# Fourier front: a root and a scaled table per tile, odd features' sums inside the eight-row products, ten tile operations on GpSimd

## The chip, the core and the metric

The program runs on one core of a Trainium2 chip. A core has engines with a queue of instructions each, which wait for one another by semaphores: TensorE (PE; its weight loads are listed as PEld) multiplies matrices into PSUM, VectorE (DVE), ScalarE (ACT) and GpSimd (POOL) work on tiles in SBUF, the first two on PSUM as well. DMAs are issued from the queues of SyncE (SP), ScalarE and GpSimd. PSUM holds eight tiles of 128x512, and a pool hands them out in turn. The metric is device time in microseconds, the median of repeated runs.

## What is computed

Two sequences of 512 rows by 1024 features pass through two layers: a Fourier mixer with an MLP, then attention with an MLP. The change touches the first mixer alone:

```python
def fourier_mix(h, w_out):
    hg = h.astype(jnp.float32).reshape(B, S, N_FGROUPS, F_GROUP)      # 8 groups of 128 features
    f = jnp.fft.fft2(hg, axes=(1, 3), norm="ortho").real
    return f.reshape(B, S, D_MODEL).astype(h.dtype) @ w_out

x = x + fourier_mix(rms_norm(x, fourier_norm[j]), fourier_w_out[j])
```

`rms_norm` divides each row by the root of its mean square and multiplies by a gain per feature.

## The kernel before, in words

The transform over positions and the one over features are products with cosine and sine tables. By symmetry of the tables an input tile of 128 rows by 1024 features (its features are laid out in two mirrored halves of 512) is replaced by the sum (`plus`) and the difference (`minus`) of its halves. A class `Front(q, c)` does this for tiles 2c and 2c+1 of sequence q: `squares` (ScalarE, sum of squares of a row), `gain` (times the gain row `gr`), `plus`, `minus`, `chain` (six small steps to the reciprocal root `r`), then scaling by `r`, and `combine`, which joins two tiles whose rows are mirrored in the sequence.

Sequence 0 comes first, with nothing to hide its start, so it uses exact f32 products: `transform(0)` multiplies three such parts (`parts[k]`: sum, difference, and a small tile for the Nyquist rows) with tables `cosX[k]`, `sinX[k]` in three rounds of `exact_even`, `exact_odd` and `exact_nyq`. `seq_evac` copies the results to SBUF, `feat_stage` multiplies by the feature tables and splits the result into a high and a low part (`split`: ScalarE copies the high half in the rounded type, VectorE subtracts it to get the low one). `an` holds the eight rows of the alternating features; `en` collects four small products (L554) for the features at multiples of 64.

The mixer's weights come as four pairs of 128x1024 tiles (`Fold`). `minus` forms their difference on VectorE, and an accumulating DMA adds the second to the first in place (L647). Differences are split into `wo` (`odd`), sums into `we` (`even_hi`, `even_lo`). `odd_outs(0)` then fills all eight PSUM tiles in four rounds over `wo`, eight outputs in each; `even_outs(0)` makes one output after another from `we[0..3]` and a small tile. Meanwhile the second sequence is prepared: `g0` and `g1` are its `Front`s, `plus_there` adds halves by an accumulating DMA on GpSimd's queue (L420), and `table(k)` loads four tables on the same queue (L329). `transform(1)` follows on TensorE, with split operands (`seq_part`, `feat_stage`), and then the same outputs for sequence 1. After it the MLP's products begin.

The order on every engine is the order of the code: the region stands under a manual schedule, and each engine runs its instructions as they are written. `idle(o, n)` puts n filler products on TensorE.

Of the kernel before, what the change touches and what calls it, by code (L numbers as in the profile page):

```python
# [44 lines left out]
def trunk_kernel(ctx, tc, x_in, xt_in, y_out, tables, rope, gfour, gcol, grow, gfin,  # L45
# [296 lines left out]
    def begin():  # L342
# [5 lines left out]
        for t in range(2, 4):  # L348
            load_x(0, t)
        exact_table(5)  # L350
        exact_table(6)
        nc.scalar.activation(one[:, :1], one[:, :1], AF.Sqrt)
        idle(ps(), 8)
        halves = []
        for i in range(2):
            o = ps()
            for k in range(4):
                c = 4 * i + k
                nc.tensor.transpose(o[:, k * P : (k + 1) * P], g[:, c : c + 1].broadcast_to([P, P]), ident)  # L359
            nc.scalar.copy(gr[:, i * 512 : i * 512 + 512], o)  # L360
            halves.append(o)
# [30 lines left out]
    def eights(x):  # L392
        return x[:, 0:512:64].unsqueeze(1).broadcast_to([P, 5, 8])

    class Front:


        def __init__(self, q, c):
            self.q, self.c = q, c
            self.ss, self.r = small(2), small(2)  # L400
            self.steps = rsqrt_steps(self.r[:, :2], self.ss[:, :2], 2, 1.0 / D)
            self.xg, self.p, self.m = [None] * 2, [None] * 2, [None] * 2
# [4 lines left out]
        def gain(self, i, k=None, o=None):  # L407
# [3 lines left out]
            nc.vector.tensor_mul(self.xg[i][:, sl], xa[self.q, 2 * self.c + i][:, sl], gr[:, sl] if o is None else o)  # L411
# [25 lines left out]
        def scale_both(self, i):  # L437
            if i == 0:
                self.n = sm.tile([P, 2, 5, 8], F32, tag="ny", name=nm("ny"), bufs=2, padded_shape=[P, 2, 8, 8])
            for out, x in ((self.p[i], self.p[i]), (self.n[:, i], eights(self.m[i])), (self.m[i], self.m[i])):  # L440
                nc.scalar.activation(out, x, AF.Copy, scale=self.r[:, i : i + 1])  # L441
            parts.append((self.p[i], self.m[i], self.n[:, i]))

        def combine(self):
            (p1, p2), (m1, m2), r, w = self.p, self.m, self.r, 8
            stt = nc.vector.scalar_tensor_tensor
            if self.q == 0:
                n = sm.tile([P, 5, 8], F32, tag="ny", name=nm("ny"), bufs=2, padded_shape=[P, 16, 8])
                stt(n, eights(m2), r[:, 1:2], eights(m1), ALU.mult, ALU.add)
# [60 lines left out]
    def exact_nyq(k, o):  # L510
        nc.tensor.matmul(o[0:40, :258], parts[k][2].rearrange("p a b -> p (a b)"), cosX[k], start=k == 0, stop=k == 2)
# [26 lines left out]
    def feat_nyq(u, j, first):  # L538
        nyt = nyqs[0][:, j * P : (j + 1) * P]
        nc.tensor.matmul(u[:, :258], nyt, an, start=first, stop=not first)  # L540
        return u

    def feat_stage(q, j, a, b, an, en, u=None):
        if q == 0:
            nc.tensor.matmul(u[:, :258], ftX[:, :P], a, start=False, stop=True)
        else:
            u = ps()
            mm3(u[:, :258], ft(0)[:, 0:P], ft(1)[:, 0:P], a[:, 0], a[:, 1], True, False)
            feat_nyq(u, j, False)
        v = ps()  # L550
        pick = slice(6 - 2 * j, 78 - 2 * j)
        if q == 0:
            nc.tensor.matmul(v[:, :256], ftX[:, P:], b, start=True, stop=True)
            nc.tensor.matmul(en[0:72, :258], pickX[:, pick], a, start=j == 0, stop=j == 3)  # L554
        else:
            mm3(v[:, :256], ft(0)[:, P:], ft(1)[:, P:], b[:, 0], b[:, 1], True, True)
            ent = tabs[2][:, 516:594][:, pick]
            nc.tensor.matmul(en[0:72, :258], ent, a[:, 0], start=j == 0, stop=False)
            nc.tensor.matmul(en[0:72, :258], ent, a[:, 1], start=False, stop=j == 3)
# [4 lines left out]

    def nyq_out(q, en):
        t = slot([P, 258], F32R)[0:72]
        nc.scalar.copy(t, en[0:72, :258])
        nc.vector.tensor_sub(t[64:72], en[64:72, :258], f32(t[64:72]))
        un[q] = t
# [9 lines left out]
    def transform(q, mid=lambda: None, hook=lambda at, j: None):  # L579
        on, ov = ps(), [(ps(), ps()) for _ in range(3)]  # L580
        if q == 0:
            for k in range(2):
                for j in range(3):
                    exact_even(k, j, ov[j][0])
                exact_nyq(k, on)
                for j in range(3):
                    exact_odd(k, j, ov[j][1])
            mid()
            exact_nyq(2, on)
        else:  # L590
            seq_nyq(q, 0, on)
            for j in range(3):
                seq_part(q, j, 0, *ov[j])
            mid()
            seq_nyq(q, 1, on)
        en = ps()
        nc.scalar.copy(an[0:40], on[0:40, :258])
        nc.vector.tensor_sub(an[32:40], on[32:40, :258], f32(an[32:40]))
        ab = []
        for j in range(3):  # L600
            if q == 0:
                exact_odd(2, j, ov[j][1])
                exact_even(2, j, ov[j][0])
            else:
                seq_part(q, j, 1, *ov[j])
            ab.append(seq_evac(q, *ov[j]))
            hook("seq", j)
        us = [None] * 4
        if q == 0:
            us[0] = feat_nyq(ps(), 0, True)  # L610
        feat_stage(q, 0, *ab[0], an, en, us[0])
        hook("feat", 0)
        o3 = ps(), ps()
        if q == 0:
            for k in range(3):
                exact_even(k, 3, o3[0])
            for k in range(3):
                exact_odd(k, 3, o3[1])
        else:
            for c in range(2):  # L620
                seq_part(q, 3, c, *o3)
        ab.append(seq_evac(q, *o3))
        hook("seq", 3)
        if q == 0:
            us[1:] = [feat_nyq(ps(), j, True) for j in range(1, 4)]
        feat_stage(q, 1, *ab[1], an, en, us[1])
        hook("feat", 1)
        feat_stage(q, 2, *ab[2], an, en, us[2])
        hook("feat", 2)
        feat_stage(q, 3, *ab[3], an, en, us[3])  # L630
        nyq_out(q, en)
        hook("feat", 3)

# [3 lines left out]
    class Fold:  # L637
# [7 lines left out]
        def minus(self):  # L645
            nc.vector.tensor_sub(self.b, self.a, self.b)
            nc.gpsimd.dma_start(self.a, w_four[1, self.j], accum_op=ALU.add)  # L647

        def odd(self):
            hi, lo = lent()  # L650
            split(hi, lo, self.b)
            wo.append((hi, lo))
# [5 lines left out]
        def even_lo(self):  # L658
            w = self.w
            nc.vector.tensor_sub(w[1], self.a, f32(w[0]))  # L660
            we[self.j] = w

    class FoldNyq:


        def __init__(self):
            self.w = slot([P, D], F32R)[0:72]
# [3 lines left out]
        def load(self):  # L671
# [7 lines left out]
            for r, i in ((0, 0), (32, 1), (64, 0)):  # L679
# [21 lines left out]
    def even_outs(q, fos):  # L701
        return outs(q, fos, we, 0, 258, (wn.w, un[q]))
# [31 lines left out]
    with tc.manual_schedule(engines={ET.PE, ET.Activation, ET.DVE, ET.Pool, ET.SP}):  # L734
        gr, halves_gr = begin()
        gc = cons.tile([P, 4 * KC], F32, name="gc")
        cosX = [exact[0][:, :258], exact[0][:, 514:772], exact[1][:, 256:514]]
        sinX = [exact[0][:, 258:514], exact[1][:, :256], exact[1][:, 514:770]]
        ftX, pickX = exact[2][:, :256], exact[2][:, 256:334]
        f0, f1, wn = Front(0, 0), Front(0, 1), FoldNyq()  # L740
        wn.load()
        idle(ps(), 28)
        f0.squares(0)
        for k in range(2):
            f0.gain(0, k, halves_gr[k])
        f0.minus(0)
        f0.plus(0)
        f0.squares(1)
        f0.gain(1, 0)
        f0.chain(0, 6)  # L750
        f0.scale_both(0)
        f0.gain(1, 1)
# [1368 lines left out]
```

## Time and profile before

| | us |
|---|---|
| median of 3 runs | 1672.69 (1672.32 to 1673.72) |
| the profiled execution's own time | 1671.97 |
| its span, first to last instruction | 1670.2 |
| TensorE busy | 1659.8 (99%) |
| VectorE busy | 1264.1 (76%) |
| ScalarE busy | 871.9 (52%) |
| GpSimd busy | 393.0 (24%) |

A row of the timeline gives the start in us from the start of the span, the duration, the engine, the line, what is written and read, and in brackets the engine's idle time ahead of it and what ended it. An f32 product counts as two instructions on TensorE (x6 is three products). Rows of neighbouring instructions are merged (x8). Names like `u`, `t`, `s` are pools: `u` the slots of 4 KB per partition, `t` the 2 KB ones, `s` small columns, `ps` PSUM.

### The profile page before, as it was taken

To read this page: it belongs to the slowest core of one execution; us is meant where nothing else is said; L and a number is where in the kernel's file an instruction comes from. 1 tells how busy PE (TensorE), PEld (TensorE's weight loads), DVE (VectorE), ACT (ScalarE), POOL (GpSimd) and SP (SyncE) were. 2 spreads that over 40 slices of the span, in tenths; PEclk is the share of its full clock that TensorE was granted. 3 is DMA by queue.
4 is the path that set the end of the run, shared out by engine and by line. 5 is a ranking of instruction groups with operands and counts; after the bars stand their busy time and mean duration, and the time that the engine had idled before them with its cause. 6 is when DMAs were issued, how large, how long until landed. Compare 5 with 4: busy or idle time off the path is not lost.

```text
span 1670.2 us, 22258 instructions
## 1 busy us (share of the span) xinstructions
PE 1659.8 (99%) x7828; PEld 1385.6 (83%) x7828; DVE 1264.1 (76%) x1851; ACT 871.9 (52%) x1540; POOL 393.0 (24%) x364
## 2 busy tenths in 40 slices
PE   9999999999999999999999999999999999999998
PEld 7988888888888888888888888888888888888887
DVE  8879776557786869869888877777855487878875
ACT  7776444446342425447688855554454552433334
POOL 3321444221000001324554303004422220000002
PEclk9999999999999999999999999999999999999999
DMA  9843555459775757425401146334544695757532
GB/s 304 259 158 115 207 192 180 145 177 370 247 232 166 247 174 230 172 77 195 161 5 38 64 177 226 114 120 171 208 146 167 223 375 193 233 157 232 183 103 101
DMA packets 122192, 302.48 MB, mean 181 GB/s; under 512 B 12344, under 2 KB 13496, under 8 KB 122080
## 3 DMA queue, kind: packets, MB, share of 16 engines
q1 hardware_dynamic: 98720, 253.53, 43.7%
q0 software_dynamic: 8960, 21.05, 5.9%
q10 hardware_dynamic: 14400, 26.48, 4.2%
q8 instruction: 61, 1.00, 0.2%
q14 instruction: 51, 0.42, 0.1%
HBM read 217.59 MB, written 82.38 MB: 180 GB/s over the span
## 4 chain that ended last, share of the span: by engine, by line
PE 98%; DVE 1%; ACT 1%; DMA 0%; issue 0%; POOL 0%; DVEq 0%; POOLq 0%
PE ps L940 75%; PE ps L83 6%; PE ps L81 6%; PE ps L82 6%; PE ps L1535 2%; PE ps L1514 0%; PE ps L191 0%; PE ps L508 0%; PE ps L505 0%; DMA g<-gfour 0%; PE ps L199 0%; ACT t L130 0%; ACT t L441 0%; DVE u L1919 0%; PE ps L359 0%
## 5 line engine op out<-in xcount | busy, mean ns | idle before, releaser
L940 PE MATMUL ps<-u,w 128*128 128x512 f32 x4944 | 1130.8, 389 | 0.0
L940 PEld LDWEIGHTS ps<-u,w 128*128 128x128 f32 x4944 | 926.8, 188 | 194.4 <-ACT u L973 1.7
L86 ACT CAST w<-raw 128x1024 fp32r<-128x1024 f32 (+1 forms) x216 | 213.6, 994 | 308.6 <-PE ps L940 230.2
L87 DVE TENSOR_TENSOR w<-raw,w 128x1024 fp32r<-128x1024 f32 (+1 forms) x216 | 251.2, 1167 | 75.6 <-ACT w L86 75.4
L86 ACT CAST u<-u 128x1024 fp32r<-128x1024 f32 x144 | 145.0, 1048 | 85.1 <-PE ps L940 37.1
L87 DVE TENSOR_TENSOR u<-u,u 128x1024 fp32r<-128x1024 f32 x144 | 173.4, 1232 | 16.9 <-ACT u L86 16.0
L940 PE MATMUL ps<-u,u 128*128 128x512 f32 x600 | 143.2, 389 | 0.0
L1150 DVE TENSOR_TENSOR u<-ps,u 128x512 f32<-128x512 f32 x160 | 109.3, 685 | 38.1 <-PE ps L940 35.6
L1177 POOL DMA_DIRECT2D raw<-w_sum x32 | 27.7, 865 | 468.9 <-DMA raw<-w_sum 158.0
L1058 POOL TENSOR_TENSOR u<-u 128x512 f32<-128x512 f32 x28 | 38.0, 1355 | 424.3 <-ACT u L955 424.3
L940 PEld LDWEIGHTS ps<-u,u 128*128 128x128 f32 x600 | 112.6, 188 | 23.8 <-ACT u L973 0.4
L81 PE MATMUL ps<-u,u 128*128 128x512 f32 (+2 forms) x340 | 128.7, 380 | 0.0
L83 PE MATMUL ps<-u,u 128*128 128x512 f32 (+2 forms) x340 | 123.7, 365 | 0.0
L82 PE MATMUL ps<-u,u 128*128 128x512 f32 (+2 forms) x340 | 123.6, 365 | 0.0
L182 POOL TENSOR_TENSOR t<-t,t 128x512 f32<-128x512 f32 (+1 forms) x54 | 79.2, 1470 | 186.7 <-ACT t L178 185.7
L954 ACT ACTIVATE t<-t 128x512 f32<-128x512 f32 x64 | 40.4, 632 | 110.0 <-DVE t L1027 100.0
L83 PEld LDWEIGHTS ps<-u,u 128*128 128x128 f32 x340 | 64.2, 189 | 10.5 <-DVE u L87 0.2
L87 DVE TENSOR_TENSOR u<-ps,u 128x512 fp32r<-128x512 f32 (+3 forms) x112 | 68.0, 634 | 5.6 <-ACT u L86 5.0
L82 PEld LDWEIGHTS ps<-u,u 128*128 128x128 f32 x340 | 64.4, 189 | 8.5 <-DVE u L87 0.3
L81 PEld LDWEIGHTS ps<-u,u 128*128 128x128 f32 x340 | 64.4, 189 | 7.8
L1014 DVE TENSOR_TENSOR t<-ps,u 128x512 f32<-128x512 f32 x32 | 22.0, 687 | 60.7 <-PE ps L940 56.9
L86 ACT CAST u<-ps 128x512 fp32r<-128x512 f32 (+3 forms) x112 | 59.2, 555 | 7.5 <-PE ps L1535 6.1
(270 smaller groups left out, 2013.7 us busy)
## 6 DMA issues: line engine op xcount, KB each, us to landing
raw<-w_up SPq DMA_DIRECT2D x80, 512.0 KB, 4.6
u<-spill_t SPq DMA_DIRECT2D x60, 512.0 KB, 7.1
raw<-w_sum SPq DMA_DIRECT2D x56, 512.0 KB, 5.6
u<-spill_b SPq DMA_DIRECT2D x45, 512.0 KB, 6.2
spill_t<-u SPq DMA_DIRECT2D x84, 256.0 KB, 2.0
spill_b<-t ACTq DMA_DIRECT2D x60, 256.0 KB, 4.3
raw<-w_row SPq DMA_DIRECT2D x28, 512.0 KB, 4.8
park<-u SPq DMA_DIRECT2D x24, 512.0 KB, 4.5
```

The costliest lines, as they stand in the source:

```text
L81: nc.tensor.matmul(out, lh, rh, start=first, stop=False)
L82: nc.tensor.matmul(out, lh, rl, start=False, stop=False)
L83: nc.tensor.matmul(out, ll, rh, start=False, stop=last)
L86: hi = nc.scalar.copy(dst_hi, src)
L87: return hi, eng.tensor_sub(dst_lo, src, f32(dst_hi))
L182: nc.gpsimd.tensor_add(acc[q][:, :n], acc[q][:, :n], s[:, :n])
L940: nc.tensor.matmul(o, w[x][:, sl], h[k][y], start=first and k + i == 0, stop=k == n - 1 and i == 2, skip_group_check=not first)
L954: nc.scalar.activation(t, src, AF.Relu)
L1058: eng.tensor_sub(t[:, 0], b12, b11)
L1150: return nc.vector.tensor_add(x, o, x)
L1177: nc.gpsimd.dma_start(s[:, 1], w[:, 3], accum_op=ALU.add)
L1535: nc.tensor.transpose(pt[:, t * P : (t + 1) * P], probs[t][:, sc * P : (sc + 1) * P], ident)
```

## The change

For the first two tiles of sequence 0 the roots are computed one by one, and each root scales its table (`exact[i]`, rows of the table belong to rows of the tile) instead of the tile's sum and difference; the tables are laid out anew so that each tile has its own. The first tile's gain is read from PSUM before the gain row is copied. All four column blocks now run in one round, so there are 4 + 4 products per round. The Nyquist tile gets 24 more columns with sums of the odd features over each group of 64 (VectorE reduces, ScalarE spreads them), so that one product of 56 rows gives both `an` and the low rows `un[0]`; the four products into `en` go for sequence 0. GpSimd multiplies the third and fourth tile of sequence 0 and all four of sequence 1 by the gain (those were VectorE's), and it adds the weights (that was a DMA). The tables of sequence 1 are loaded later in the code, fold tiles and inputs earlier; twelve and twenty fillers replace eight and 28.

```diff
-        idle(ps(), 8)
+        idle(ps(), 12)
...
-            nc.scalar.copy(gr[:, i * 512 : i * 512 + 512], o)
...
+    def nyq_tiles(n):
+        t = sm.tile([P, n, 2, 4, 8], F32, tag="ny", name=nm("ny"), bufs=2, padded_shape=[P, 2, 2, 4, 8])
+        return [t[:, i] for i in range(n)]
+    def odd_sums(k):
+        s = small(8)
+        x = parts[k][0].rearrange("p (g d i) -> p g d i", g=8, i=2)[:, :, :, 1]
+        nc.vector.tensor_reduce(s, x, AX.X, ALU.add)
+        return s
+    def put_sums(k, s):
+        nc.scalar.copy(parts[k][2][:, :, 1:], s.unsqueeze(1).unsqueeze(1).broadcast_to([P, 2, 3, 8]))
...
-            nc.vector.tensor_mul(self.xg[i][:, sl], xa[self.q, 2 * self.c + i][:, sl], gr[:, sl] if o is None else o)
+            eng.tensor_mul(self.xg[i][:, sl], xa[self.q, 2 * self.c + i][:, sl], gr[:, sl] if o is None else o)
...
-            for out, x in ((self.p[i], self.p[i]), (self.n[:, i], eights(self.m[i])), (self.m[i], self.m[i])):
-                nc.scalar.activation(out, x, AF.Copy, scale=self.r[:, i : i + 1])
+        def table(self, i):
+            t = exact[i][:, :514]
+            nc.scalar.activation(t, t, AF.Copy, scale=self.r[:, i : i + 1])
...
+    def put_low(on):
+        norm = 1.0 / math.sqrt(S * P)
+        low = slot([P, 258], F32R)[0:56]
+        nc.scalar.activation(low, on[0:56, :258], AF.Copy, scale=norm)
+        nc.vector.scalar_tensor_tensor(low[32:56], on[32:56, :258], norm, f32(low[32:56]), ALU.mult, ALU.subtract)
+        un[0] = low
...
+    def transform_exact(mid, hook):
+        ov = [(ps(), ps()) for _ in range(4)]
+        for k in range(2):
+            for j in range(4):
+                exact_even(k, j, ov[j][0])
+            for j in range(4):
+                exact_odd(k, j, ov[j][1])
+        mid()
+        ab = []
+        for j in range(4):
+            exact_odd(2, j, ov[j][1])
+            exact_even(2, j, ov[j][0])
+            ab.append(seq_evac(0, *ov[j]))
+            hook("seq", j)
+        on = ps()
+        for k in range(3):
+            exact_nyq(k, on)
+        put_an(on)
+        put_low(on)
...
-            nc.vector.tensor_sub(self.b, self.a, self.b)
-            nc.gpsimd.dma_start(self.a, w_four[1, self.j], accum_op=ALU.add)
+            nc.vector.tensor_sub(self.d, self.a, self.b)
+        def plus(self):
+            nc.gpsimd.tensor_add(self.a, self.a, self.b)
...
-        idle(ps(), 28)
+        idle(ps(), 20)
+        f0.table(0)
...
+        f1.gain(0, eng=nc.gpsimd)
+        f1.gain(1, eng=nc.gpsimd)
...
+        for i in range(2):
+            g0.gain(i, eng=nc.gpsimd)
+        for j in range(4):
+            fold[j].even_hi()
         fold[0].even_lo()
         fold[1].even_lo()
+        g0.minus(1)
+        g0.plus_there(1)
+        fold[2].even_lo()
+        fold[3].even_lo()
+        g1.gain(0, eng=nc.gpsimd)
...
+        g1.gain(1, eng=nc.gpsimd)
...
         even(0)
+        g0.combine()
+        g0.split_even()
+        g0.split_odd()
...
         g1.minus(1)
         g1.plus_there(1)
+        for k in range(4):
+            table(k)
```

Where instructions move, engine by engine. VectorE in the front, from the first tile's sum on (`t_199`/`t_205` is a sum, `u_203`/`u_248` the second tile times its gain, `s` the root's small columns). Before:

```order
L415 TENSOR_TENSOR t_199<-u_194 128x512
L411 TENSOR_TENSOR u_203<-u_104,u_99 128x512
L141 TENSOR_SCALAR s_141<-s_139 128x2
L143 RECIPROCAL s_142<-s_143 128x2
L144 TENSOR_TENSOR s_144<-s_142 128x2
L145 SCALAR_TENSOR_TENSOR s_144<-s_144,s_141 128x2
L146 SCALAR_TENSOR_TENSOR s_140<-s_144,s_142 128x2
L411 TENSOR_TENSOR u_203<-u_104,u_99 128x512
```

And now:

```order
L146 SCALAR_TENSOR_TENSOR s_140<-s_144,s_142 128x1
L433 TENSOR_TENSOR t_205<-u_193 128x512
L442 TENSOR_TENSOR t_207<-u_193 128x512
L429 TENSOR_TENSOR u_248<-u_104,u_99 128x1024
L141 TENSOR_SCALAR s_145<-s_139 128x1
L143 RECIPROCAL s_146<-s_147 128x1
L144 TENSOR_TENSOR s_148<-s_146 128x1
L145 SCALAR_TENSOR_TENSOR s_148<-s_148,s_145 128x1
L146 SCALAR_TENSOR_TENSOR s_140<-s_148,s_146 128x1
L433 TENSOR_TENSOR t_262<-u_248 128x512
```

The first root stands ahead of the first tile's sum and difference, and the second root behind the second tile's whole gain product.

VectorE between the last odd weights and the first even output (`w` are the even weights' low halves, `t_416`/`t_540` and `t_423`/`t_560` the differences of the second sequence's first two tiles). Before:

```order
L87 TENSOR_TENSOR u_409<-u_301,u_408 128x1024
L411 TENSOR_TENSOR u_414<-u_304,u_99 128x1024
L424 TENSOR_TENSOR t_416<-u_414 128x512
L411 TENSOR_TENSOR u_421<-u_306,u_99 128x1024
L424 TENSOR_TENSOR t_423<-u_421 128x512
L141 TENSOR_SCALAR s_244<-s_242 128x2
L143 RECIPROCAL s_245<-s_246 128x2
L144 TENSOR_TENSOR s_247<-s_245 128x2
L145 SCALAR_TENSOR_TENSOR s_247<-s_247,s_244 128x2
L146 SCALAR_TENSOR_TENSOR s_243<-s_247,s_245 128x2
L660 TENSOR_TENSOR w_536<-raw_234,w_536 128x1024
L660 TENSOR_TENSOR w_538<-raw_238,w_538 128x1024
```

And now:

```order
L689 TENSOR_TENSOR u_425<-u_418,u_424 128x1024
L442 TENSOR_TENSOR t_540<-u_432 128x512
L141 TENSOR_SCALAR s_160<-s_158 128x2
L143 RECIPROCAL s_161<-s_162 128x2
L144 TENSOR_TENSOR s_163<-s_161 128x2
L145 SCALAR_TENSOR_TENSOR s_163<-s_163,s_160 128x2
L146 SCALAR_TENSOR_TENSOR s_159<-s_163,s_161 128x2
L701 TENSOR_TENSOR w_550<-raw_221,w_550 128x1024
L701 TENSOR_TENSOR w_552<-raw_227,w_552 128x1024
L442 TENSOR_TENSOR t_560<-u_434 128x512
L701 TENSOR_TENSOR w_554<-raw_231,w_554 128x1024
L701 TENSOR_TENSOR w_556<-u_235,w_556 128x1024
```

The gain products (L411) left VectorE; the differences that read them stayed ahead of the even halves, the second one between them.

GpSimd's queue from the weights to the tables (`raw` are weight tiles, `u_414`, `u_421` and now `u_432` to `u_573` the second sequence's tiles, `dcos` and the rest its tables). Before:

```order
L647 DMA raw_296<-w_four 128x1024
L647 DMA u_300<-w_four 128x1024
L420 DMA u_414<-u_414 128x512
L420 DMA u_421<-u_421 128x512
L431 TENSOR_TENSOR s_544<-s_243,mask 128x1
L455 MEMSET ny_570 128x128
L329 DMA u_579<-dcos 128x774
L329 DMA u_581<-dsin 128x1024
```

And now:

```order
L429 TENSOR_TENSOR u_434<-u_241,u_99 128x1024
L438 DMA u_432<-u_432 128x512
L449 TENSOR_TENSOR s_548<-s_159,mask 128x1
L438 DMA u_434<-u_434 128x512
L429 TENSOR_TENSOR u_565<-u_243,u_99 128x1024
L429 TENSOR_TENSOR u_573<-u_245,u_99 128x1024
L438 DMA u_565<-u_565 128x512
L476 MEMSET ny_607 128x128
L438 DMA u_573<-u_573 128x512
L329 DMA u_630<-dcos 128x774
L329 DMA u_632<-dsin 128x1024
```

The four adds of weights (L682) and the second sequence's first product (L429) stand ahead of these rows. The tables now come behind all four gain products and all four adds of halves.

More of the change, by code (lines that the diff above doesn't have):

```diff
@@ L577, in idle, with put_an @@
             nc.tensor.matmul(o[:, :256], filler, filler.unsqueeze(1).broadcast_to([P, 2, P]), start=True, stop=True)
[L579 to L596, printed above, removed]
+    def put_an(on):
@@ L792, in hook0 @@
             elif j == 3:
+                fold[3].minus()
+                fold[3].plus()
+                g0.squares(1)
+                g0.chain(1, 2)
                 fold[3].odd()
[L794 to L803 removed]
+        transform_exact(mid, hook0)
```

303 lines of the change are left out of this document (154 added, 149 removed).

## The prediction

> **What bounds the kernel now.** I read the page first, then the list of what TensorE (PE) waits for, then busy time by stage, then the order of time of single engines.
>
> ```profile
> span 1670.2 us, 22258 instructions
> PE 98%; DVE 1%; ACT 1%; DMA 0%; issue 0%; POOL 0%; DVEq 0%; POOLq 0%
> ```
>
> ```profile
> PE ps L505 <- ACT t L441: 1.4, 2, 1.0
> ```
>
> ```profile
> 0.00:10.60 10.60, 7.81 (x45) 7.35 (x45) 4.99 (x18) 5.82 (x11) 1.84 (x8) 1.00 0.81 313
> 10.60:29.55 18.95, 18.55 (x82) 13.75 (x83) 18.68 (x30) 14.67 (x33) 8.16 (x10) 1.00 1.04 372
> 29.55:41.26 11.71, 11.71 (x99) 11.68 (x98) 10.77 (x18) 10.01 (x18) 5.54 (x9) 1.00 1.01 189
> 41.26:54.00 12.74, 12.74 (x109) 12.73 (x108) 12.13 (x25) 9.85 (x31) 4.16 (x6) 1.00 0.67 160
> ```
>
> The chain that ends last is PE for 98%. In the Fourier front PE waits 1.4 us for scaled sums and from then on for nothing. The windows give length, then busy time of PE, weight loads, DVE (VectorE), ACT (ScalarE), POOL (GpSimd). VectorE is busy 18.68 of 18.95 us, 10.77 of 11.71 and 12.13 of 12.74: the second limit lies right behind the first. So whatever holds VectorE up in the first 57 us moves PE; after the front the program is PE-bound and its order unchanged, so a shift at the second transform stays to the end.
>
> ```profile
> 1.18 2.07 PE L577 MATMUL ps<-u 128*128 128x256 f32 x8 [1.18 <-DVE mask L370]
> 3.84 1.94 PE L359 MATMUL ps<-ident,g 128*128 128x128 f32 x8 [0.59 <-DMA g<-gfour]
> 5.43 4.15 PE L577 MATMUL ps<-u 128*128 128x256 f32 x28
> 10.60 1.57 PE L505 MATMUL ps<-u,t 128*128 128x258 f32 x6 [1.01 <-ACT t L441]
> ...
> 22.87 1.47 PE L505 MATMUL ps<-u,t 128*128 128x258 f32 x6
> 24.17 1.46 PE L508 MATMUL ps<-u,t 128*128 128x256 f32 x6
> ...
> 29.55 0.47 PE L81 MATMUL ps<-u,u 128*128 128x256 f32 x1
> ...
> 41.26 0.28 PE L81 MATMUL ps<-u,w 128*128 128x258 f32 x1
> ...
> 42.71 0.28 PE L698 MATMUL ps<-u,u 72*128 72x258 f32 x1
> ...
> 53.75 0.28 PE L81 MATMUL ps<-u,ny 128*40 128x258 f32 x1
> ```
>
> These are my checkpoints: first exact product 10.60, first odd output 29.55, first even output 41.26, end of that output 42.8, second transform 53.75. Three exact products take 1.30 us (22.87 to 24.17), one 0.43.
>
> **PE's own work.** Twelve fillers stand ahead of the transposes instead of eight: about 0.9 us more, which fills the 0.59 us wait, so the transposes come some 0.1 later. Twenty follow instead of 28; eight fast ones less, at the 0.12 us of the 96 products between 29.55 and 41.26, are 1.0 less, so PE is free at 9.6+0.1-1.0 = 8.7. The scaled table is there by then:
>
> ```profile
> 7.16 0.69 DVE L424 TENSOR_TENSOR t<-u 128x512 f32<-128x512 f32 x1
> 7.77 0.69 DVE L415 TENSOR_TENSOR t<-u 128x512 f32<-128x512 f32 x1
> 17.67 0.75 DVE L450 SCALAR_TENSOR_TENSOR t<-t,s,t 128x512 f32<-128x512 f32 x1
> 28.31 2.07 DVE L87 TENSOR_TENSOR u<-ps,u 128x257 fp32r<-128x257 f32 x6
> 36.21 0.16 DVE L141 TENSOR_SCALAR s<-s 128x2 f32<-128x2 f32 x1
> 36.94 3.49 DVE L660 TENSOR_TENSOR w<-raw,w 128x1024 fp32r<-128x1024 f32 x3
> 40.66 1.23 DVE L660 TENSOR_TENSOR w<-u,w 128x1024 fp32r<-128x1024 f32 x1 [0.23 <-ACT w L656]
> ```
>
> ```profile
> 9.82 0.72 ACT L441 ACTIVATE t<-t,s 128x512 f32<-128x512 f32 x1 [1.00 <-DVE s L146]
> ```
>
> The first half of the transposes ends near 5.0 (3.84, half of 1.94, and 0.1). VectorE's half products need no copy first and end at 5.8 and 6.6, the root's steps take 0.73 (36.21 to 36.94), the scaling 0.72: ready near 8.0. Start of the exact products: 10.60 to 8.7, **-1.9**. They number 35 instead of 39 (four e/n products, L554, go): **-1.7**; the second wait of 0.4 goes. Unhindered, odd outputs would begin near 25.5.
>
> **GpSimd's tiles and the shared access.** Ten 128x1024 products or adds of two SBUF tiles move to GpSimd: two in front, four for the weights, four for the second sequence. In front of them on its queue only memsets are left. No 128x1024 stands in the trace; these rows bound it.
>
> ```profile
> L1488 POOL TENSOR_TENSOR t<-u,u x4: 732/734/742, 865.7 to 888.7; 128x256 f32<-128x256 f32 x4
> ```
>
> ```profile
> L182 POOL TENSOR_TENSOR t<-t,t 128x512 f32<-128x512 f32 x48 | 73.3, 1530 | 179.6 <-ACT t L178 178.7
> ```
>
> ```profile
> 287.61 1.28 POOL L1059 TENSOR_TENSOR u<-t,u 128x512 f32<-128x512 f32 x1
> ```
>
> ```profile
> 156.40 1.29 POOL L1058 TENSOR_TENSOR u<-u 128x512 f32<-128x512 f32 x1 [54.43 <-ACT u L955]
> 157.77 1.62 POOL L1059 TENSOR_TENSOR u<-t,u 128x512 f32<-128x512 f32 x1
> 159.35 1.74 POOL L1060 TENSOR_TENSOR u<-t,u 128x512 f32<-128x512 f32 x1
> ```
>
> ```profile
> 157.13 1.11 DVE L989 TENSOR_TENSOR raw<-raw,raw 128x512 f32<-128x512 f32 x1
> 158.27 1.67 DVE L990 TENSOR_TENSOR raw<-raw 128x512 f32<-128x512 f32 x1
> 159.86 0.68 DVE L1027 TENSOR_TENSOR t<-ps,t 128x512 f32<-128x512 f32 x1
> ```
>
> 0.73 for 256 and 1.28 for 512 elements, so 0.55 per 256: 2.4 for 1024 (ends: 1.3, one 512 row, and 3.1, twice L182's mean; I take the value on the line through the two uncrowded rows). The last two fences interlock. VectorE's L989, of a shape that takes 0.69 (L424), ends at 158.24, 0.55 after GpSimd's first add ends (157.69). GpSimd's second ends at 159.39, 1.15 after L989. L990 ends at 159.94, again 0.55 after. L1027, one operand from PSUM, runs beside an add at its 0.68. So a VectorE operation with both operands in SBUF and a GpSimd one exclude each other, in order of asking, but for a lead of 0.14. A moved tile holds VectorE's two-operand work off for up to 2.26, twice what its own 128x1024 costs ((3.49-1.22)/2 = 1.14). The trace shows 512 columns; I take the whole instruction for 1024 too. [...]
>
> **The sum, checkpoint by checkpoint** (0.60 per 128x512 on VectorE, 0.67 with a scalar, 0.345 per PSUM split, 1.14 per 128x1024):
>
> *Front to the odd outputs.* VectorE forms the first tile's sum and difference by 8.5 (7.3 and two of 0.60). From there to the last sum of the third round VectorE has one 1.14, six 0.60, two 0.67, two roots and a small sum: 8.2, so 16.6 without GpSimd. The two tiles of 2.26 come between, about 1.2 of them beside root steps, which have no two large operands: 19.9. PE, ready at 15.8, waits some 3.4. Behind three reductions (0.4 each) and two weight differences (2.3) the first two weight adds on GpSimd end at 27.8; the first odd lower half, queued behind, ends at 28.8, the splits at 29.5. First odd output 29.5: the 4.0 saved are spent, **0.0**.
>
> *Odd outputs.* The third result's bank is freed by a split that now stands behind an odd half and a weight difference (29.5+1.2+1.1+0.3 = 32.1; PE is there at 30.1: +2.0). The seventh's stands behind the third add, which ends at 34.2, and an odd half: 35.6, +2.0. First even output 41.26 to 45.3: **+4.0**.
>
> *First even output.* VectorE's queue holds the second sequence's difference ahead of all four even halves, and that waits for GpSimd. The fourth odd half ends at 40.5; then GpSimd's two tiles run on end to 45.1; difference 0.6, root 0.7, two halves 2.3, difference 0.6, third half 1.1: 50.4; GpSimd's next tile holds access to 52.6; fourth half 53.7. End of the output 54.1 instead of 42.8: **+11.3** in all. Before, the fourth half ended at 41.9.
>
> *To the second transform.* Seven more even outputs, 1.56 each (42.71 on): 65.0.
>
> ```profile
> 38.31 1.70 POOL L329 DMA_DIRECT2D u<-dcos  x1
> 41.20 0.54 POOL L329 DMA_DIRECT2D u<-dfeat  x1
> 45.74 0.88 POOL L420 DMA_DIRECT2D u<-u  x1 [4.01 <-DVE t L424]
> ```
>
> ```profile
> u<-dcos POOLq DMA_DIRECT2D x1, 387.0 KB, 4.8
> ```
>
> The tables were issued at 38.3, 15 us ahead of use. Now they stand behind the last add of halves, which waits for a VectorE difference that stands behind the first even output's add, combine and splits (54 to 61.2); 0.9 for its issue, then 4.8: 66.9, +1.9. Behind the tables two input DMAs (0.9 each) and the memset for the second eight-row tile follow, and the even adds that free PSUM banks wait behind that: some 2 more. I take **+4.0** (ends 1 and 6). The fold's four accumulating DMAs go; PE's list of waits names none of them, so that gains nothing. ScalarE loses four scalings and gains two tables and three small copies; it is behind VectorE in every window, so I cost it at nothing (if it were the limit, a scaling is 0.72).
>
> Sum: +15.3. The span becomes 1685.5 against 1670.2; that execution took 1671.97 and the runs' median is 1672.69, so I add to the median: **1688.0 us**.
>
> **Rivals.**
> *No exclusion (0.17).* GpSimd's and VectorE's passes share access at 1024 columns. The same walk without blocks starts odd outputs at 24.8, yet the first even output still waits for a tile behind the adds, and tables still come late: +5, 1677.6. Against it: every crowded row above.
> *The clock falls (0.20).* The first eight fillers take 2.07 us where later ones need 0.12 each, so TensorE starts at half speed. In the walk PE works under a third of the time from 44 to 54. Nothing in before shows such a gap. Two stretches of 3 us at half speed once work is there again cost 1.5 each: +18.3, 1691. [...]
> *GpSimd hides (0.08).* A tile takes 1.3 or less and VectorE, rid of six 1.14 products, keeps ahead. Then 1.9+1.7+0.4 stays: 1668.7. It decides where the second sequence's first tile is done before the odd outputs end (near 37). Against it: the 256 and 512 rows already give 0.55 per 256.
> *The earlier start fails* (a late tile or root): VectorE's queue ends the waits anyway, so the sum hardly changes.
>
> **How the numbers follow.** The forecast has 0.50 (1683 to 1692); 0.05 lies between no exclusion and no change. Low is the no-exclusion case less 2, 1675.5; high is a 3.1 us tile's share (ten tiles by 0.7, half of it on the path, +3.5) with part of the clock's loss: 1694. Within 0.2% is 3.3 us, about what runs of this kernel can tell: faster 0.08, same 0.05, slower 0.87.
>
> **What would show it.** Right: VectorE two-operand rows of over 2 us beside GpSimd's 128x1024 rows near 2.4 to 3.5; first exact product near 8.7; first odd output near 29.5; first even output ending near 54; waits of PE's even products for L701 halves, and of VectorE's difference for GpSimd's L429; the tables issued after 60. Wrong: VectorE's 128x1024 rows all near 1.22, or the first even output ending before 45.

## The result, and the profile after

The changed kernel takes 1696.51 us (median of 4, 1694.94 to 1697.31) against 1673.20 for the kernel before (4 runs): a ratio of 1.0137, 95% interval 1.0125 to 1.0150, so 23.3 us slower. The forecast was 1688.0 with a range up to 1694: the direction was right, the loss half as large again as said, and outside the range. The profiled execution spans 1693.2 us against 1670.2. One run of the last kernel below (1847.63 us) and one of the kernel before beside it (2077.74) ran at a lower granted clock throughout (0.85 and 0.75) and are left out of all medians and ratios.

The chain of the kernel after that ended last, between 36 and 60 us (start, length, engine, tile, line):

```profile
37.69 2.42 POOL u L682
40.11 3.35 POOL u L429
...
43.49 2.87 DVE t L442
...
47.09 2.27 DVE w L701 x2
...
49.96 6.96 DVE w L701 x2
...
56.97 0.58 PE ps L83
```

The list of what TensorE waits for up to 115 us (total, times, longest):

```profile
PE ps L83 <- DVE w L701: 8.2, 4, 4.8
PE ps L81 <- DVE u L87: 4.1, 3, 1.9
PE ps L526 <- ACT u L457: 3.7, 2, 3.4
PE ps L598 <- DVE mask L368: 1.2, 1, 1.2
```

GpSimd's tiles (L682, L429) and VectorE's two-operand work (L442, L701) take turns, and TensorE hangs on the end of the row: 8.2 us for the even halves. The first line names the even halves' subtraction (L701), the second the splits that free PSUM tiles (L87), the third the scaled tables of the front (L457). No row names a table of the second sequence or a transfer. The same checkpoints on TensorE as in the prediction:

```profile
15.03 0.80 PE L526 MATMUL ps<-u,t 128*128 128x258 f32 x1 [3.40 <-ACT u L457]
...
29.81 0.35 PE L81 MATMUL ps<-u,u 128*128 128x256 f32 x1 [0.53 <-DVE u L87]
...
45.65 0.28 PE L81 MATMUL ps<-u,w 128*128 128x258 f32 x1
...
57.48 0.58 PE L741 MATMUL ps<-u,u 56*128 56x258 f32 x1
...
73.53 0.31 PE L81 MATMUL ps<-u,ny 128*40 128x258 f32 x1
...
113.91 0.40 PE L1002 MATMUL ps<-u,w 128*128 128x512 f32 x1
```

The last checkpoint, the first product of the MLP, stands in the kernel before at:

```profile
91.04 0.40 PE L940 MATMUL ps<-u,w 128*128 128x512 f32 x1
```

| stretch | forecast, us | profile, us |
|---|---|---|
| to the first odd output | 0.0 | +0.3 |
| odd outputs | +4.0 | +4.1 |
| first even output, to its end | +7.3 | +10.7 |
| seven more even outputs, to the second transform | +4.0 | +4.7 |
| second transform and its outputs, to the MLP | 0 | +3.1 |
| MLP and all behind | 0 | +0.1 |
| sum | +15.3 | +23.0 |

Two things in it were not in the walk. The first is the granted clock. The windows of the kernel after (length; busy time of PE, weight loads, DVE, ACT, POOL; then the clock, DMA share, GB/s):

```profile
47.60:51.00 3.40, 1.66 (x6) 1.14 (x6) 3.40 (x4) 1.71 (x6) 1.40 (x3) 0.67 0.45 77
51.00:54.50 3.50, 1.01 (x3) 0.71 (x3) 3.50 (x2) 3.50 (x10) 3.50 (x3) 0.50 0.44 75
...
57.90:61.30 3.40, 3.40 (x14) 2.94 (x13) 3.00 (x7) 1.77 (x5) 1.09 (x2) 0.50 0.47 81
61.30:64.70 3.40, 3.40 (x21) 3.06 (x21) 2.69 (x6) 1.91 (x7) 0.84 (x2) 0.84 0.01 1
```

TensorE is busy 1.66 of 3.40 us, then under a third of the time, and the clock falls to 0.50; it stays there through a full window of work and comes back during the one after (0.84 in its mean). The second: an even output takes longer even at full clock. First the kernel after, with the small product of 56 rows (L741) and its neighbours; then the kernel before, with 72 rows (L698):

```profile
65.22 0.28 PE L83 MATMUL ps<-u,w 128*128 128x258 f32 x1
65.43 0.38 PE L741 MATMUL ps<-u,u 56*128 56x258 f32 x1
65.74 0.39 PE L81 MATMUL ps<-u,w 128*128 128x258 f32 x1
65.97 0.28 PE L82 MATMUL ps<-u,w 128*128 128x258 f32 x1
...
67.38 0.38 PE L741 MATMUL ps<-u,u 56*128 56x258 f32 x1
```

```profile
44.15 0.28 PE L83 MATMUL ps<-u,w 128*128 128x258 f32 x1
44.27 0.28 PE L698 MATMUL ps<-u,u 72*128 72x258 f32 x1
44.39 0.28 PE L81 MATMUL ps<-u,w 128*128 128x258 f32 x1
```

Neighbours at full clock start 0.12 apart. Around the 56 rows the starts are 0.21, 0.31 and 0.23 apart: 0.39 more, 1.95 per output instead of 1.56. The 48 rows of the second sequence cost the same (starts at 88.79, 89.00, 89.31 and 89.54), and 16 outputs make 6.2 us. No engine waits in it, so no list of waits shows it; only the rows of the two kernels side by side do.

### The profile page after: what moved, and what is told of

It reads as the page before. It is cut to its first block, busy times and chain, and to the rows that moved or that the text cites. A ratio compares the mean times of both kernels' runs of the same rounds, so it can differ in the third digit from the quotient of the medians.

```text
span 1693.2 us, 22245 instructions
## 1 busy us (share of the span) xinstructions
PE 1668.8 (99%) x7816; PEld 1389.5 (82%) x7816; DVE 1272.5 (75%) x1852; ACT 871.5 (51%) x1542; POOL 413.5 (24%) x370
## 4 chain that ended last, share of the span: by engine, by line
PE 95%; DVE 1%; POOL 1%; issue 1%; DMA 0%; ACT 0%; SPq 0%; DVEq 0%; POOLq 0%
PE ps L1002 74%; PE ps L81 6%; PE ps L83 6%; PE ps L82 6%; PE ps L1597 2%; DVE w L701 1%; POOL u L429 1%; PE ps L1576 0%; POOL raw L682 0%; PE ps L191 0%; DMA u<-x 0%; PE ps L741 0%; DVE t L442 0%; PE ps L199 0%; POOL u L682 0%
## 5 line engine op out<-in xcount | busy, mean ns | idle before, releaser
L87 DVE TENSOR_TENSOR w<-raw,w 128x1024 fp32r<-128x1024 f32 (+1 forms) x216 | 251.8, 1169 | 75.9 <-ACT w L86 75.7
L86 ACT CAST u<-u 128x1024 fp32r<-128x1024 f32 (+1 forms) x140 | 140.7, 1046 | 87.4 <-PE ps L1002 39.8
L87 DVE TENSOR_TENSOR u<-u,u 128x1024 fp32r<-128x1024 f32 (+1 forms) x140 | 169.4, 1240 | 16.7 <-ACT u L86 16.0
L81 PEld LDWEIGHTS ps<-u,u 128*128 128x128 f32 x340 | 64.4, 189 | 12.6 <-DVE u L87 4.0
L87 DVE TENSOR_TENSOR u<-ps,u 128x512 fp32r<-128x512 f32 (+3 forms) x112 | 68.2, 635 | 5.6 <-ACT u L86 5.1
L82 PEld LDWEIGHTS ps<-u,u 128*128 128x128 f32 x340 | 64.4, 189 | 8.6 <-DVE u L87 0.3
L1591 POOL TENSOR_SCALAR t<-t,s 128x512 f32<-128x512 f32 x64 | 45.4, 710 | 73.4 <-DVE s L1590 60.1
```

Of the source, the lines that this page charges most:

```text
L81: nc.tensor.matmul(out, lh, rh, start=first, stop=False)
L82: nc.tensor.matmul(out, lh, rl, start=False, stop=False)
L86: hi = nc.scalar.copy(dst_hi, src)
L87: return hi, eng.tensor_sub(dst_lo, src, f32(dst_hi))
L1591: nc.gpsimd.tensor_scalar(p, p, sm_[:, :1], 1.0, ALU.mult, ALU.mult)
```

## The experiments

In brackets behind each run: its median in us, its ratio to the kernel before, measured beside it (1672.95 to 1673.46), and the 95% interval. "Less" and "faster" are against the change's 1696.51 unless another kernel is named. The change's own four runs spread by 2.4 us. In the profiles of all these kernels the transposes wait for the gain row's DMA and start at 4.36 to 4.75 us, in the change's at 3.97, so places in them can lie some 0.4 to 0.8 later for that reason alone; and from the MLP's first product to the end the profiles differ by up to 1.8 us (1579.1 to 1580.9) although that code is the same.

**Rows of the small product** (1693.48; ratio 1.0119, 1.0104 to 1.0134). 

```diff
-            self.w = slot([P, D], F32R)[0:56]
+            self.w = slot([P, D], F32R)
...
-        return outs(q, fos, we, 0, 258, (wn.w[: 48 if q else 56], un[q]))
+        return outs(q, fos, we, 0, 258, (wn.w[:72], un[q]))
```

> The changed kernel, with the small product at the end of each even output over 72 rows again (zero weights in the added rows) instead of 56 and 48; nothing else moves but one filler ahead of the eight-row products (0.16 us). Theory A, 64 rows or fewer cost TensorE a change of its arrangement: the product's row falls from 0.38 to 0.28 us and an even output from 1.95 to 1.56, 16 times 0.39 = 6.2 us in all; 1690.5 us, or up to 3 more if the late tables take the place of the first sequence's share. Theory B, the 0.39 comes from the slow clock or from neighbours in SBUF: 1.95 stays, 1696.5.

An output takes 1.56 again, in both sequences. From the end of the first even output to the MLP it is 51.8 us (58.83 to 110.67) instead of 55.85, 4.0 less. The median falls by 3.0, at the lower edge of what was expected: the outputs behind the first run at half clock for longer (0.50 and 0.56 in the windows from 57.9 to 64.7 us, 0.50 and 0.84 in the change), and a wait of 1.0 for a PSUM tile that ScalarE frees (L772) takes a part.

**A ladder of rows** (one run).

```diff
-        return outs(q, fos, we, 0, 258, (wn.w[: 48 if q else 56], un[q]))
+        n = ((72, 65, 64, 56, 64, 65, 72, 48) if q else (72, 72, 56, 64, 65, 72, 96, 128))[fos[0]]
+        return outs(q, fos, we, 0, 258, (wn.w[:n], un[q][:n]))
```

> The small product of the even outputs runs over a different number of rows (zero rows added) in each output: 72, 72, 56, 64, 65, 72, 96, 128 in the first sequence and 72, 65, 64, 56, 64, 65, 72, 48 in the second. Theory A, the price belongs to row counts up to 64: outputs of 48, 56 and 64 rows take 1.95 and those of 65, 72, 96 and 128 rows 1.56, in both sequences. Theory B, the price grows with fewer rows or belongs to rows that are no multiple of 32: 64, 96 and 128 would be the cheap ones, 65 and 72 dear.

The small products of the first sequence, from its third output on:

```profile
62.77 0.38 PE L742 MATMUL ps<-u,u 56*128 56x258 f32 x1
64.73 0.38 PE L742 MATMUL ps<-u,u 64*128 64x258 f32 x1
66.59 0.28 PE L742 MATMUL ps<-u,u 65*128 65x258 f32 x1
68.16 0.28 PE L742 MATMUL ps<-u,u 72*128 72x258 f32 x1
...
71.28 0.28 PE L742 MATMUL ps<-u,u 128*128 128x258 f32 x1
```

1.96 between two small ones, 1.86 on the way out (the 0.1 ahead of the product is missing), then 1.56 and 1.57. The price ends between 64 and 65 rows; the second sequence shows the same steps. Theory B falls.

**The second sequence's gain products back on VectorE** (1689.49; 1.0099, 1.0082 to 1.0116).

```diff
-            g0.gain(i, eng=nc.gpsimd)
+            g0.gain(i)
...
-        g1.gain(0, eng=nc.gpsimd)
+        g1.gain(0)
...
-        g1.gain(1, eng=nc.gpsimd)
+        g1.gain(1)
```

> The changed kernel with the second sequence's four gain products on VectorE again, at the same places of the code. Theory A, VectorE's difference and even halves wait for GpSimd's tiles and for access to SBUF: the end of the first even output falls from 58.1 to about 50.5, PE's wait for the halves (8.2 us) to about 3, the granted clock stays at 1.00 after 48 us; 1688.5 us (1687 to 1691). Theory B, GpSimd's tiles are hidden and VectorE's own load sets the end: four products of 1.14 more on VectorE make it 1699 to 1701.

VectorE takes on four products of 1.14 and the kernel gets 7.0 faster. TensorE waits 2.1 for the halves instead of 8.2. The last half, which takes 5.90 in the change, takes 1.22:

```profile
49.42 1.22 DVE L701 TENSOR_TENSOR w<-u,w 128x1024 fp32r<-128x1024 f32 x1
```

Against the expectation the clock still falls (0.50 from 51.0 to 54.5 us): the next two outputs take 3.39 and 3.14. The first one ends at 51.79, where 50.5 was expected.

**The first sequence's two gain products back on VectorE** (1694.91; 1.0127, 1.0112 to 1.0142).

```diff
-        f1.gain(0, eng=nc.gpsimd)
-        f1.gain(1, eng=nc.gpsimd)
...
         f0.minus(1)
+        f1.gain(0)
...
             put_nyq()
+            f1.gain(1)
```

> The changed kernel with the gain products of the third and fourth tile of the first sequence on VectorE. Theory A, access to SBUF is exclusive: the small steps of the second tile's root take 0.16 each instead of 2.06 and 2.26, PE's second table wait of 3.4 falls to about 1, the first odd output comes at 28.2 instead of 29.8, and of this some 1.5 us reach the end, since later waits for GpSimd's weight adds take the place; 1695 us. Theory B, the small steps were slow for another reason (ScalarE's table, the clock): they stay over 2 us and the time rises by the two 1.14 products, 1698 to 1699.

The second root's steps in the changed kernel, and in this one:

```profile
9.59 2.06 DVE L144 TENSOR_TENSOR s<-s 128x1 f32<-128x1 f32 x1
11.68 2.26 DVE L145 SCALAR_TENSOR_TENSOR s<-s,s 128x1 f32<-128x1 f32 x1
```

```profile
10.43 0.16 DVE L144 TENSOR_TENSOR s<-s 128x1 f32<-128x1 f32 x1
10.62 0.16 DVE L145 SCALAR_TENSOR_TENSOR s<-s,s 128x1 f32<-128x1 f32 x1
```

Theory A holds in the steps. The second table wait is gone, but TensorE waits 2.9 for the third tile instead, and the first odd output comes at 30.09 rather than the 28.2 expected. The median falls by 1.6, as theory A has it, but the two intervals overlap, and in the profile the MLP's first product comes only 0.35 earlier: that time is gained isn't shown clearly. Theory B's 1698 to 1699 falls.

**The weights' adds as accumulating DMAs** (1692.84; 1.0116, 1.0101 to 1.0131).

```diff
-            nc.gpsimd.tensor_add(self.a, self.a, self.b)
+            nc.gpsimd.dma_start(self.a, w_four[1, self.j], accum_op=ALU.add)
```

> The changed kernel with the four adds of weights as accumulating DMAs again. Theory A (exclusive access): the odd halves beside the adds take 1.2 instead of 2.3 us, the splits that free PSUM banks come earlier, the first even output starts at about 42 instead of 45.6, and 4 to 6 us reach the end: 1691 to 1692.5. Theory B, the adds are hidden under PE's products: 1696.5, or more if the accumulating DMAs land late.

The time is close to theory A (3.7 less, 4 to 6 expected), the place is not: the even output starts at 46.27, since the second sequence's first two tiles come earlier on GpSimd and hold the fourth odd half up for both:

```profile
37.48 6.00 DVE L689 TENSOR_TENSOR u<-u,u 128x1024 fp32r<-128x1024 f32 x1 [1.11 <-ACT u L686]
```

**TensorE kept busy in the wait** (1694.95; 1.0131, 1.0116 to 1.0146).

```diff
+                    nc.tensor.matmul(o[i], wh, u[:, 1], start=False, stop=False)
+                    for _ in range(warm[k]):
+                        nc.tensor.matmul(full[0][:, 260:], filler, filler[:, :126].unsqueeze(1).broadcast_to([P, 2, 126]), start=False, stop=False)
+                    nc.tensor.matmul(o[i], wl, u[:, 0], start=False, stop=False)
```

> The changed kernel with 18, 4, 6 and 36 filler products on TensorE between the second and the third product of the four steps of the first even output, where it waits for the halves (2.2, 0.5, 0.7 and 4.8 us). Theory A, the granted clock falls because TensorE idles there: it stays at 1.00 from 47 to 65 us, the two even outputs after the first take 1.95 each instead of 3.39 and 2.61, and the first one ends some 0.5 earlier; 2.6 us less, 1694. Theory B, the clock has another cause or the fillers delay the work: 1696.5 or more.

```profile
54.50:57.90 3.40, 2.33 (x21) 2.13 (x19) 3.40 (x2) 1.56 (x5) 2.17 (x1) 1.00 0.00 0
57.90:61.30 3.40, 3.40 (x22) 2.88 (x23) 3.14 (x8) 1.35 (x4) 1.11 (x2) 1.00 0.37 64
```

The clock stays at 1.00 in every window from 44 to 65 us, where the change has 0.50 to 0.84 from 47.6 to 64.7, and the outputs behind take 1.95 each: here TensorE's idle time is the cause. In the profile the second transform starts 1.4 earlier than in the change (72.12), TensorE, early now, waits 0.8 there for a copy of ScalarE's, and the MLP's first product comes 0.3 earlier. The median falls by 1.6 of the 2.6 expected, but the intervals overlap: how much reaches the end isn't shown clearly.

**A memset between GpSimd's last two tiles** (1696.33; 1.0137, 1.0123 to 1.0151).

```diff
+        nc.gpsimd.memset(small(8), 0.0)
         g1.gain(1, eng=nc.gpsimd)
```

> The changed kernel with one memset of a small column tile on GpSimd between the third and the fourth gain product of the second sequence. Theory A, in the changed kernel GpSimd's fourth tile begins before the third has ended and takes the access ahead of VectorE's last even half, which waits for both (5.90 us); with the memset between them VectorE gets its turn: that half takes 3.6, the first even output ends 2.3 earlier, 1694.2 us. Theory B, the half loses its turn because it asks just after GpSimd began, whatever follows: 5.9 stays, 1696.5.

Theory B's number: VectorE's half takes 5.94, as in the change. GpSimd's two tiles of that kernel and the half:

```profile
51.95 2.63 POOL L429 TENSOR_TENSOR u<-u,u 128x1024 f32<-128x1024 f32 x1
54.31 0.31 POOL L882 MEMSET s<- 128x8 f32 x1
54.38 2.54 POOL L429 TENSOR_TENSOR u<-u,u 128x1024 f32<-128x1024 f32 x1
```

```profile
52.07 5.94 DVE L701 TENSOR_TENSOR w<-u,w 128x1024 fp32r<-128x1024 f32 x1
```

VectorE asks at 52.07, 0.12 after GpSimd began, and passes only when the second tile is done (56.92). The memset too begins 0.27 ahead of the first tile's end, so the early start that theory A blames may still be it; a longer gap was not tried. Theory B's reason is not enough by itself (below).

**The even halves ahead of the second sequence on VectorE** (1696.47; 1.0140, 1.0125 to 1.0156).

```diff
-        g0.minus(0)
-        g0.plus_there(0)
-        g0.chain(0, 1)
-        g0.chain(2, 6)
         for j in range(4):
             fold[j].even_hi()
...
+        for j in range(4):
+            fold[j].even_lo()
+        g0.minus(0)
+        g0.plus_there(0)
+        g0.chain(0, 1)
+        g0.chain(2, 6)
```

> The changed kernel with VectorE's four even halves ahead of the second sequence's differences and root. Theory A, the halves are late only because the head of VectorE's queue waits for a GpSimd tile: the first even output ends near 51 instead of 58.1, but the second sequence's steps and the tables, issued after them on GpSimd, come later, and 3 to 7 us are given back before the second transform: 1690 to 1696.5. Theory B, nothing is given back: 1689.5.

The first even output ends at 51.86, 6.2 earlier, and everything is given back, the upper end of theory A. Theory B falls. TensorE's list of waits now has rows that the change's does not:

```profile
PE ps L81 <- DMA u<-dcos: 1.8, 1, 1.8
PE ps L81 <- ACT u L765: 1.5, 1, 1.5
...
PE ps L81 <- ACT u L771: 1.0, 1, 1.0
```

**No tile on GpSimd, 72 rows** (1684.61; 1.0071, 1.0056 to 1.0086): the edits above for all ten tiles and for the rows, in one kernel.

> The changed kernel without any of the ten tile operations on GpSimd (gain products on VectorE, adds of weights as accumulating DMAs) and with small products of 72 rows; the places of the tables' loads and of the second sequence's steps stay as changed. Theory A, GpSimd's tiles and the rows are nearly all of the loss: the first odd output comes near 27.5, the first even output ends near 45; then the tables, loaded behind the second sequence's adds, become the next wait, up to 6 us at the second transform: 1677 to 1681. Theory B, nothing waits for the late tables: 1673 to 1675.

11.9 us less than the change, but more than expected remains (1677 to 1681). The first odd output still comes at 30.82, the first even output ends at 48.90, and TensorE waits 2.1 for the first table (`dcos`) and 1.1 for ScalarE. So the late tables, hidden in the change, do cost time once what stands ahead of them is faster.

**The new front with the old order behind it** (1676.04; 1.0019, 1.0009 to 1.0028): as the last kernel, and from the first odd output on the code of before, tables included; the third and fourth weight differences are earlier.

> The new front alone: a root and a scaled table per tile, the odd sums in the small product, small products of 72 rows, no tile on GpSimd; from the first odd output on the steps stand as before the change, tables included, and the differences of the weights are put where VectorE would idle. Theory A, VectorE is the second limit right behind TensorE: the odd outputs start 2 earlier, near 27.3, but wait some 2.8 for splits, the first even output starts at 41.5 and the time is before's, 1672.5 to 1674.5. Theory B, the 3.6 us that TensorE saves in front reach the end: 1669 to 1670.

Nearer to theory A, but above its range: 8.6 us less again, from the order alone, yet 3.0 over the kernel before (1673.08 beside it), and the first odd output at 29.66, not 27.3. In the profile the MLP's first product comes 2.85 later than before; 2.7 of it arise in the odd outputs, which take 14.41 instead of 11.71 with three waits for splits (2.1 in all). TensorE idles 3.1 for the third tile's parts and loses its clock in the products behind:

```profile
13.50:16.90 3.40, 2.08 (x10) 1.49 (x8) 3.26 (x9) 1.69 (x3) 0.94 (x1) 1.00 1.04 416
16.90:20.30 3.40, 1.66 (x4) 1.27 (x5) 3.37 (x9) 0.15 (x1) 0.00 (x0) 0.78 1.02 408
```

**The same with fillers in that wait** (1675.79; 1.0014, 1.0005 to 1.0022).

```diff
+        for _ in range(22):
+            nc.tensor.matmul(ov[3][0][:, 260:], filler, filler[:, :126].unsqueeze(1).broadcast_to([P, 2, 126]), start=False, stop=False)
         mid()
...
-        put_low(on)
         hook("an", 0)
+        put_low(on)
```

> The kernel of the old order with the new front (1676.0), with 22 filler products on TensorE where it waits 3.1 us for the third tile's parts, and the first odd half ahead of the low rows' subtraction on VectorE. Theory A, the wait drops the granted clock and the eight products and copies behind it run late, which VectorE then waits for (2.5 us): with the clock at 1.00 the first odd output comes near 28 instead of 29.7 and 1.5 to 2.5 us reach the end: 1673.5 to 1674.5, before's time. Theory B, VectorE sets the end alone: 1676.

The clock stays at 1.00, the first odd output comes at 28.44 and the MLP's first product 1.3 earlier in the profile; the median falls by 0.25 only, inside the spread of these runs (1673.35 to 1676.85). Theory B is nearer in time, but not shown: the profile has the gain in front of the MLP, and the odd outputs still wait 2.1 for VectorE's splits.

**The rows alone** (1680.82; 1.0042, 1.0028 to 1.0055): the last kernel with 56 and 48 rows again.

> The kernel before this one (the new front with TensorE kept busy, the old order, no tile on GpSimd: 1675.8), with small products of 56 and 48 rows as in the change instead of 72. No wait stands at the second transform here that could take the place. Theory A, 16 switches at 0.39 reach the end whole: 6.0 to 6.2 us more, 1682.0. Theory B, a part is hidden wherever another engine is behind, as it was with all of GpSimd's tiles: 3 us more, 1679.

```profile
44.11 0.28 PE L81 MATMUL ps<-u,w 128*128 128x258 f32 x1
...
100.03 0.40 PE L1006 MATMUL ps<-u,w 128*128 128x512 f32 x1
```

```profile
42.84 0.28 PE L81 MATMUL ps<-u,w 128*128 128x258 f32 x1
...
92.63 0.40 PE L1007 MATMUL ps<-u,w 128*128 128x512 f32 x1
```

From the first even output to the MLP 55.92 us with 56 and 48 rows (first fence), 49.79 with 72: 6.13, nearly the whole 6.2 of 16 products. The medians differ by 5.0, less than theory A's 6.0 to 6.2 and more than theory B's 3; the runs of the two kernels spread by 1.6 and 3.5.

None of these kernels beats the kernel before.

## Why the prediction was wrong, point by point

- **TensorE's own work: the step that failed.** The prediction counted the products that go and did not look at the shape of one that stays. The small product shrinks from 72 rows to 56 and 48, in both sequences. The term was 0 and is 16 times 0.39, 6.2 us; the ladder and the rows alone show it (6.13 in the profile, 5.0 in the medians). It is the whole +3.1 behind the second transform and 2.7 of the +4.7 ahead of it. What the traces show is the 0.39 for each such product and the edge between 64 and 65 rows; the "change of its arrangement" in the first expectation was the author's guess at a reason, and no run shows one.
- **First even output: the mechanism right, the last tile mis-sized.** The walk let the fourth half in after one GpSimd tile ("GpSimd's next tile holds access to 52.6; fourth half 53.7"). It was held over two and ended at 56.92. That is 3.2 later, 0.7 of it inherited from the fourth odd half (41.2 instead of 40.5). The last two products at half clock (0.50 until 62.41) add some 0.7; against that the stretch began 0.35 later than forecast (45.65) and its base, taken as 42.8, was 43.0. Together they are the 3.4 missing in this stretch.
- **The clock.** It was a rival at 0.20, with +3; it came. In the profile the two outputs behind the wait cost 3.39 and 2.61 instead of 1.95, 2.1 in all; kept up, the second transform starts 1.4 earlier. The fall came after 3.41 us (45.34 to 48.75) in which TensorE was busy 1.19 and idle for at most 2.22 on end. No run shows the rival's two stretches of 3 us at half speed: in the change the clock is 0.50 for 13.66 us (48.75 to 62.41), and TensorE was busy 7.64 of them.
- **To the second transform: +4.0 for late tables, near the measured 4.7 by luck.** TensorE waited for no table there. The 4.7 are the clock's 2.1 and seven small products (2.7). The tables were late (issued at 64.4, forecast "after 60") but everything else was later still; with the halves first or without GpSimd's tiles they do end a wait (1.8 and 2.1).
- **Front and odd outputs: right in size, 0.3 and 4.1 for 0.0 and 4.0.** The odd outputs' two waits (1.75 and 1.86) are those of the walk, before the third and the seventh output. In the front the 3.4 of waiting came elsewhere: not ahead of the third tile's parts but ahead of the second table (15.03, 3.40), so the size there is in part luck; the first exact product came at 7.89, not 8.7. One reason in it was wrong: the root's steps, "which have no two large operands", are blocked too (2.06 and 2.26). It was not felt, since VectorE's queue ends the waits either way, as the rival on a failing earlier start had it. Putting these two tiles back lowers the median by 1.6, not clear of the spread.
- **The exclusion itself: right.** A GpSimd tile alone takes 2.39 and 2.42 in the change, where 2.4 was forecast, VectorE's tile rows beside them 2.25 to 2.87 and once 5.90, and the kernels that take the second sequence's tiles or the weights' adds off GpSimd gain 7.0 and 3.7. The rivals without exclusion and with GpSimd hidden fall.
- **The sum.** Without the tables' 4.0, and with 6.2 for the rows, 2.4 for the second tile and 2 to 3 for the clock, the forecast's terms come to 22 to 23; 23.0 was measured. (The no-exclusion rival's +5 makes 1677.7, not the 1677.6 written there.)

## What to carry to other kernels

When a change shrinks a matrix product, compare its row count with those of its neighbours: here 56 rows among products of 128 cost 0.39 us each time, and zero rows up to 72 cost nothing. Before moving two-operand tile work from VectorE to GpSimd, ask what VectorE does meanwhile: here a tile cost GpSimd 2.4 us and kept VectorE's two-operand work waiting for up to 2.2 (the 2.87 at 43.49 instead of 0.68), or over two tiles for 4.7 (5.90 instead of 1.22), against 1.14 for doing it itself. And a saving ahead of an engine that is the second limit is spent there: in the new front with the old order TensorE, started 2 us earlier, idled 3.1 for VectorE and lost its clock (0.78 from 16.9 to 20.3 us).

## What the runs showed of the hardware that was not expected

- TensorE: a product over 48, 56 or 64 rows among products over 128 rows adds 0.39 us in all at full clock (0.09 ahead of it, 0.30 behind: 65.22 to 65.97 in the change for 56 rows, 88.79 to 89.54 for 48, 64.51 to 65.26 in the ladder for 64); over 65, 72, 96 or 128 rows it adds nothing (66.59, 68.16, 69.72 and 71.28 in the ladder, the next product 0.12 to 0.13 later). A product with 40 output columns adds nothing either (in the kernel before the second transform's first starts at 53.75 and the next 0.12 later).
- Exclusive access holds for VectorE operations of 128x1 too (2.06 and 2.26 us beside GpSimd's first two tiles, 0.16 without them), and it isn't always in order of asking. In the change and in the kernel with the memset VectorE passed only after two GpSimd tiles (5.90 and 5.94 us); with the weights' adds as DMAs two more halves take as long (6.00 and 6.03). In the change and with the memset VectorE had asked 0.12 after the first tile began (51.01 and 50.89, 52.07 and 51.95), and GpSimd's next instruction began 0.25 and 0.27 before that tile's end; in three places of the change where VectorE passed after one tile and another instruction followed on it, that began 0.04 to 0.05 before its end (11.59, 13.89, 40.06). The time of asking alone doesn't decide: in the change VectorE asked 0.09 after a tile began (11.68 and 11.59) and passed after that one. The two waits for two tiles have one more thing in common: the first tile begins 0.26 ahead of the end of a DMA issue on GpSimd's own queue (50.89 and 51.15, 51.95 and 52.21). Whether the DMA issue decides was not tried.
- The granted clock in the change is 0.50 from 14.62 to 18.04 and from 48.75 to 62.41 us. These four changes lie 3.42, 30.71 and 13.66 us apart: one, nine and four times 3.413, to 0.01. TensorE was busy 0.42 of the 3.41 us ahead of the first fall and 1.19 of those ahead of the second; after 1.69 (31.69 to 35.10) the clock stayed at 1.00, and in the second fence below it fell after 1.78. The stretches of the odd outputs' waits in the kernel with fillers and 72 rows, then in the one with 56 and 48 (the first one's stretches are an estimate: reckoned back from its only change, at 1670.74, in steps of 3.413):

```profile
28.93:32.35 3.42, 2.13 (x16) 1.73 (x14) 3.42 (x7) 3.42 (x7) 0.80 (x1) 1.00 1.11 219
32.35:35.76 3.41, 2.59 (x22) 2.39 (x21) 3.41 (x5) 3.38 (x7) 0.11 (x1) 1.00 1.05 221
```

```profile
29.96:33.38 3.42, 1.78 (x12) 1.37 (x12) 3.42 (x7) 3.42 (x7) 0.91 (x1) 1.00 1.08 213
33.38:36.79 3.41, 3.41 (x17) 3.41 (x17) 3.38 (x5) 2.46 (x5) 0.00 (x0) 0.50 1.05 220
```

  Both kernels have the same three waits (0.47, 0.82 and 0.82). In the first they lie two and one in the two stretches, and the clock stays at 1.00; in the second the last two lie in one stretch, and the clock behind it is 0.50. That this alone decides isn't shown.
